# The first down-projection product of an encoder trunk: its right factors loaded anew for each of the seven products, and the attention carried on beside four of them

## The chip, the core and the metric

The kernel runs on one core of one Trainium2 chip. The metric is the device time in microseconds (us) of the whole program. Matmuls run on PE, elementwise work with two operands on DVE and POOL, activations and casts on ACT; SP issues nearly all DMAs. Each engine takes its own instructions strictly in the order in which they stand in its queue, and waits at an instruction until the semaphores that it needs are there. That order is written by the build: the kernel's Python yields pieces of work, two generators are woven into each other by weights, and a scheduler places the instructions of that stream into the five queues.

## The reference, cut to what matters

One layer, sequence of 2048 tokens, width 1024, float32:

```
h = rmsnorm(x); proj = h @ w_in
y_a = s5_mixer(..)            # state space
y_b = diff_attention(..)      # 6 heads, two softmax maps each, causal by chunks of 64
y_c = hgrn2_mixer(..)         # gated linear recurrence, 6 heads
x = x + concat(y_a, y_b, y_c) @ w_out
h = rmsnorm(x)
up = causal_conv3(h @ w_up) + conv_b; gate = h @ w_gate
x = x + (gelu(up) * gate) @ w_down      # 2816 -> 1024
return rmsnorm(x)
```

Every float32 matmul is done as three float16 matmuls on a high and a low half (the helper `split`: ACT makes the high half, DVE or POOL subtracts it for the low half).

## The kernel before, in words

**Stages.** In order of time: the input projection and the S5 part; then the gated recurrence (hgrn, tiles `g_...`) with the first rows of the attention beside it; `early_mix` (`o_pe`), a part of the output projection; and `phase_tail`, which works on two halves of 1024 tokens each. For the first half the tail does the output projection (`project`, `o_pm`), the normalisation and transposes (`o_pt`), the up and gate products (`activations`, `f_pm`, 1848 matmuls), and the down-projection (`Down`, `f_pd`). Then `second` does the output projection of the second half, `activations` and `Down` follow for it, and the program ends.

**The attention.** `phase_attn` is called twice: for query blocks 0 to 7, and for blocks 8 to 15 (the "second part"). One row is one block of 128 queries of one head. A row with block number i has L = 128(i+1) keys. Its steps: score matmuls `t_ps` (PE, line 834, 3 or 4 per map in the second part, two maps), a biased copy with running maximum on DVE (line 838, one for each `t_ps`), the exponentials on ACT (line 850, two of 128 x L), the difference of the two maps on DVE (line 869), the cast on ACT (line 892), the low half on POOL (line 893), two transposing DMAs on SP (line 900, `t_wt`), and the value matmuls `t_po` (PE, line 915, 64 columns each, three for each block of 128 keys). The second part has 48 rows and 336 `t_ps`.

**The weave.** `weave(fore, 1.0, right(), 1.0)` draws from the attention (`left`) or from all else (`right`), whichever has the smaller account. A piece of the attention's second part adds its n times `LW[4]` times `K.pace`; a piece of the tail adds n times `LW[5]` = 1. `K.pace` is 1.0 at first, 1.8 from the output projection on, and is set again where `activations` begins. `run(fore)`, handed down as `ahead`, draws what is left of the attention at one go.

**The down-projection.** `Down` computes (1024 x 2816) @ (2816 x 1024) as seven products of half size (a Strassen-like scheme). Product i needs a left factor (sums of the activations, written to the DRAM tensor `Ad` by `factors`, read back as `f_da` by `left`) and a right factor (a sum of the four quarters B11, B12, B21, B22 of `w_down`, split into the float16 pair `f_dw`). A product runs over four parts c of 3, 3, 3 and 2 blocks (`DOWN_PARTS`), 36, 36, 36 and 24 matmuls, 132 in all, into four PSUM banks; at its end `put` adds them to the rows `f_r` on DVE (line 1750). There are six buffers for parts of right factors, so one and a half products are held at a time.

For the first half (`staged` = 4) the right factors of products 0 to 3 come by `stage`: the quarter is loaded in pieces of at most two blocks into the pool `f_dst` (3 buffers of 512 KB), for product 3 two quarters are loaded and subtracted on POOL, then split. Ahead of product 2, `before()` draws the rest of the attention, and `hold` opens the pool `f_db` for the four whole quarters. They are loaded there (line 1726), and products 4 to 6 form their factors from what lies there, each sum overwriting one quarter (lines 1730 and 1733, POOL). Product 6 of the first half is left to `second`. For the second half all right factors come from held quarters.

**Lines that the prediction touches.** 834, 838, 850, 869, 892, 893, 900, 915: a row of the attention. 98: the `f_pm` matmuls. 60 and 58: the low half of an activation factor `f_a` on DVE and on POOL. 62: the low half of a weight. 1705 and 1726: loads into `f_dst` and `f_db`. 1743: load of `f_da`. 1772: the `f_pd` matmuls. 1837: the helper `add`.

Of the kernel before, what the change touches and what calls it, by code (L numbers as in the profile page):

```python
# [26 lines left out]
CH = 512  # L27
# [9 lines left out]
LW = [6.0, 0.44, 5.0, 2.5, 0.62, 1.0]  # L37
# [1383 lines left out]
def phase_tail(K, x, Xd, Yd, Ad, w_out, norm_g, W, conv_w, conv_b, w_down, final_g, out, es,  # L1421
# [228 lines left out]
    class Down:  # L1650
# [19 lines left out]
        LOADS = ({2: (B12, B11), 3: (B22,), 4: (B21,)}, {0: (B21,), 1: (B22, B11), 2: (B12,)})  # L1670
# [22 lines left out]
        def stage(self, i, st, cs=(0, 1, 2, 3)):  # L1693

            for c in cs:
                q0, n = self.cuts[c]
                w = self.room(i, c)
                for q in range(0, n, 2):
                    k = min(2, n - q)
                    b, pair, _ = self.STEPS[i]  # L1700
                    fs = []
                    for b in pair or (b,):
                        f = st.tile([128, KD, 128], F32, tag="wst", name="f_dst")
                        f = f.rearrange("p (q a) f -> p q (a f)", q=2)[:, 0:k]
                        nc.sync.dma_start(out=f, in_=self.source(b, q0 + q, k))
# [96 lines left out]
        def run(self, rs, tp, pms, side, staged, before):  # L1802
# [3 lines left out]
            with ExitStack() as e1:  # L1806
                pool = pooler(e1)
                st = pool("f_dst", 3) if staged > 1 else None
                self.more(pool)
                if not self.w:  # L1810
                    self.ahead(st)
                with ExitStack() as e2:
                    for i in range(6):
# [3 lines left out]
                        if i == staged - 1 - (staged > 1):  # L1817
                            before()
                            self.hold(pooler(e2)("f_db", 1, side))
                        for b in self.LOADS[self.half].get(i, ()):  # L1820
                            self.load(b)
                        if i + 1 < staged:
                            self.stage(i + 1, st)
                        else:
                            for c in range(len(self.cuts)):
                                if i + 1 == staged == 4:
                                    self.sum(3, c)
                                self.right(i + 1, c)
# [3 lines left out]
                if self.half == 1:  # L1832
                    yield from self.product(6, pms[6 % len(pms)], True)
            self.last = self.product(6, pms[0], False)
# [76 lines left out]
    def first(pm):  # L1911

        with ExitStack() as e1:
# [22 lines left out]
            K.pace = 1.0  # L1936
# [45 lines left out]
    with ExitStack() as e2:  # L1982
# [7 lines left out]
        yield from down.run(total(0), tp, [pm], "left", 4, ahead)  # L1990
# [9 lines left out]
    yield from down.run(total(1), tp, [pd, pm], "left", 1, lambda: None)  # L2000
# [117 lines left out]
```

## Time and profile before

| what | value |
|---|---|
| median of 3 runs | 2815.44 us (2808.53 to 2818.59) |
| the profiled execution: time | 2795.69 us |
| the profiled execution: span of the instructions | 2794.0 us |
| mean granted clock of PE | 0.931 of full speed |

The page gives shares of the whole span. For this change the shares of single stages count, and those come from the view that cuts the span into windows. In its rows stand the length of the window, the busy time of each engine with the number of its instructions in brackets, the granted PE clock, the mean busy share of the DMA engines and the GB/s that they moved. Matmuls overlap: one of 512 columns is recorded with about 0.38 us, but the next starts about 0.22 us after it, so the rate is read from counts in a window.

### The profile page before, as it was taken

To read this page: it belongs to the slowest core of one execution; us is meant where nothing else is said; L and a number is where in the kernel's file an instruction comes from. 1 tells how busy PE (TensorE), PEld (TensorE's weight loads), DVE (VectorE), ACT (ScalarE), POOL (GpSimd) and SP (SyncE) were. 2 spreads that over 40 slices of the span, in tenths; PEclk is the share of its full clock that TensorE was granted. 3 is DMA by queue.
4 is the path that set the end of the run, shared out by engine and by line. 5 is a ranking of instruction groups with operands and counts; after the bars stand their busy time and mean duration, and the time that the engine had idled before them with its cause. 6 is when DMAs were issued, how large, how long until landed. Compare 5 with 4: busy or idle time off the path is not lost. (4 is left out here: it accounts for less than half of the span.)

```text
span 2794.0 us, 42749 instructions
## 1 busy us (share of the span) xinstructions
PE 2442.0 (87%) x15438; PEld 1375.0 (49%) x15438; DVE 2004.2 (72%) x3893; ACT 1222.2 (44%) x2231; POOL 1309.4 (47%) x1095
## 2 busy tenths in 40 slices
PE   5998897989988888677998887859899999999998
PEld 3654546867766764243443333324344444444443
DVE  7466746789988897688779899975654855555575
ACT  5333344556645663565345555552234422222221
POOL 4788602334334432246666666631802344444180
PEclk8999998989989988788999999979999999999999
DMA  6675554555464656864455655587775655554733
GB/s 226 232 219 192 162 174 101 123 131 132 90 150 98 132 130 134 253 171 120 164 172 158 175 140 159 142 256 239 258 268 192 221 164 154 166 155 143 270 103 121
DMA packets 554533, 474.13 MB, mean 170 GB/s; under 512 B 276880, under 2 KB 432848, under 8 KB 553296
## 3 DMA queue, kind: packets, MB, share of 16 engines
q1 hardware_dynamic: 532144, 431.02, 54.1%
q10 hardware_dynamic: 22176, 40.38, 4.0%
q8 instruction: 121, 1.98, 0.3%
q14 instruction: 92, 0.75, 0.1%
HBM read 289.30 MB, written 127.93 MB: 149 GB/s over the span
## 5 line engine op out<-in xcount | busy, mean ns | idle before, releaser
L98 PE MATMUL f_pm<-f_q,f_w 128*128 128x512 f16 x3696 | 841.3, 387 | 37.9 <-DVE f_u L1837 21.7
L98 PEld LDWEIGHTS <-f_w 128*128 128x128 f16 x3696 | 363.7, 99 | 506.7 <-issue 90.4
L1772 PE MATMUL f_pd<-f_dw,f_da 128*128 128x512 f16 x1848 | 406.5, 383 | 11.7 <-DVE f_r L1750 10.4
L893 POOL TENSOR_TENSOR t_sc<-t_sc 128x1024 f16<-128x1024 f32 (+7 forms) x144 | 250.2, 1749 | 338.9 <-ACT t_sc L892 313.5
L1772 PEld LDWEIGHTS <-f_da 128*128 128x128 f16 x1848 | 181.8, 99 | 233.0 <-issue 18.5
L850 ACT ACTIVATE t_sc<-t_sc,t_nm 128x128 f32<-128x128 f32 (+7 forms) x192 | 229.1, 1195 | 99.1 <-DVE t_nm L845 91.7
L834 PE MATMUL t_ps<-t_k,t_q 96*128 96x512 f16 (+2 forms) x480 | 168.7, 377 | 99.0 <-DVE t_mx L838 86.6
L838 DVE CUSTOM_DVE_ANT_0 t_sc<-t_ps,t_base,t_mx 128x512 f32<-128x512 f32 (+3 forms) x288 | 185.1, 643 | 28.2 <-PE t_ps L834 21.5
L60 DVE TENSOR_TENSOR f_a<-f_t,f_a 128x512 f16<-128x512 f32 x132 | 148.1, 1129 | 46.1 <-ACT f_a L54 42.0
L98 PE MATMUL g_pq<-g_h,g_w 128*128 128x256 f16 x1152 | 158.6, 298 | 16.7 <-DVE g_sg L1162 10.6
L915 PE MATMUL t_po<-t_v,t_wt 128*128 128x64 f16 x2448 | 123.2, 201 | 56.4 <-DMA t_wt<-t_sc 48.7
L915 PEld LDWEIGHTS <-t_wt 128*128 128x128 f16 x2448 | 109.2, 104 | 123.1 <-DMA t_wt<-t_sc 67.0
L1837 POOL TENSOR_TENSOR f_t<-f_t,f_t 128x512 f32<-128x512 f32 x66 | 106.8, 1632 | 129.3 <-ACT f_a L54 108.3
L1487 PE MATMUL o_pm<-o_w,o_y 128*128 128x512 f16 x624 | 147.1, 394 | 19.9 <-DMA o_y<-Yd 14.1
L869 DVE SCALAR_TENSOR_TENSOR t_sc<-t_sc,t_a 128x1024 f32<-128x1024 f32 (+7 forms) x144 | 163.2, 1159 | 0.9
L1837 POOL TENSOR_TENSOR f_k<-f_k,f_k 128x512 f32<-128x512 f32 x88 | 124.7, 1417 | 73.2 <-ACT f_k L1869 68.3
L98 PE MATMUL g_pv<-g_w,g_h 128*128 128x256 f16 x1152 | 151.5, 288 | 8.0 <-ACT g_w L54 4.7
L62 DVE SCALAR_TENSOR_TENSOR f_dw<-f_db,f_dw 128x1536 f16<-128x1536 f32 (+1 forms) x36 | 104.1, 2910 | 73.8 <-ACT f_dw L54 73.7
L1837 POOL TENSOR_TENSOR f_db<-f_db 128x1536 f32<-128x1536 f32 (+1 forms) x32 | 128.2, 4044 | 60.6 <-DMA f_db<-in_w_down_dram 60.6
L892 ACT CAST t_sc<-t_sc 128x1024 f16<-128x1024 f32 (+7 forms) x144 | 112.1, 793 | 93.1 <-DVE t_sc L869 89.5
L54 ACT ACTIVATE f_w<-f_sum 128x512 f16<-128x512 f32 x110 | 69.2, 629 | 182.4 <-DVE f_sum L141 76.9
L54 ACT ACTIVATE f_a<-f_t 128x512 f16<-128x512 f32 x154 | 95.5, 628 | 114.5 <-POOL f_t L1837 56.6
(327 smaller groups left out, 4534.8 us busy)
## 6 DMA issues: line engine op xcount, KB each, us to landing
f_w<-Wd SPq DMA_DIRECT2D x231, 256.0 KB, 3.0
Wd<-f_w SPq DMA_DIRECT2D x154, 256.0 KB, 2.1
Ad<-f_a ACTq DMA_DIRECT2D x154, 256.0 KB, 2.8
f_da<-Ad SPq DMA_DIRECT2D x42, 768.0 KB, 4.4
g_h<-Hd SPq DMA_DIRECT2D x24, 1024.0 KB, 7.0
f_db<-in_w_down_dram SPq DMA_DIRECT2D x24, 768.0 KB, 10.5
o_wst<-in_w_out_dram SPq DMA_DIRECT2D x32, 512.0 KB, 5.4
o_y<-Yd SPq DMA_DIRECT2D x52, 256.0 KB, 4.7
```

Of the source, the lines that this page charges most:

```text
L54: nc.scalar.activation(out=hi, in_=src, func=AF.Copy, scale=scale)
L60: nc.vector.tensor_tensor(out=lo, in0=src, in1=hi, op=ALU.subtract)
L98: nc.tensor.matmul(out=out, lhsT=lhs(a, k), rhs=rhs(b, k), start=(n == 0), stop=(n == 3 * nk - 1))
L834: nc.tensor.matmul(out=ps[:, 0:k1 - k0], lhsT=qt[:, c, 128 * (i % 4):128 * (i % 4) + 128], rhs=H.k[:, c, k0:k1], start=True, stop=True,)
L838: V.tensor_tensor_reduce(out=sc[c][:, k0:k1], in0=ps[:, 0:k1 - k0], in1=bs[:, k0:k1], scale=1.0, scalar=-3e38 if j == 0 else mx[:, c, j - ...
L850: nc.scalar.activation(out=sc[c][:, 0:L], in_=sc[c][:, 0:L], func=AF.Exp, scale=SLOPES[h], bias=nm[:, c:c + 1], accum_out=H.la[:, c, n_:n_ ...
L869: V.scalar_tensor_tensor(out=sc[0][:, k0:k1], in0=sc[1][:, k0:k1], scalar=a[:, 1:2], in1=sc[0][:, k0:k1], op0=ALU.mult, op1=ALU.add,)
L893: nc.gpsimd.tensor_tensor(out=hl[:, LM + k0:LM + k1], in0=sc[0][:, k0:k1], in1=hl[:, k0:k1], op=ALU.subtract,)
L915: nc.tensor.matmul(out=po, lhsT=wt[:, w, b, :], rhs=vt[:, b, 64 * v:64 * v + 64], start=(b == 0 and w + v == 0), stop=(b == i and w == 1),)
L1487: nc.tensor.matmul(out=ps[t], lhsT=y[:, k, a, 128 * t:128 * t + 128], rhs=w[:, b, k, :], start=(q == qs[0] and i == 0), stop=(q == qs[-1] ...
L1772: nc.tensor.matmul(out=ps[t], lhsT=a[:, q, x, tk], rhs=w[:, y, q, :], start=(first and q + x + y == 0), stop=(last and q == n - 1 and y == 1),
L1837: eng.tensor_tensor(out=o, in0=a, in1=b, op=op)
```

## The change

`Down.run` is parted in two. The first half's product gets its own function `streamed`: all seven right factors come by `stage`, in pieces, from `w_down`. The table `SUMS` says which quarters a factor is made of: one for products 0, 1, 2, two for 3 and 4, three for 5. For product 5 the sum is kept as one tile (`f_db`, a quarter of the space that `hold` took), and product 6 takes its factor from that and B21. The pool `f_dst` has 4 buffers instead of 3. The rest of the attention is drawn ahead of product 4 instead of product 2. Quarters read for the first half: 11 instead of 9 (each 1408 x 512 float32, 2.88 MB). The second half's `run` is as before with the cases for the first taken out. `LW[4]` goes from 0.62 to 0.72, and `K.pace` beside `activations` from 1.0 to 0.86, so that their product there stays (0.619 for 0.62), while beside the recurrence and the output projection the attention's account grows faster.

```diff
-LW = [6.0, 0.44, 5.0, 2.5, 0.62, 1.0]
+LW = [6.0, 0.44, 5.0, 2.5, 0.72, 1.0]
...
+        SUMS = (
+            (B11,), (B21,), (B22,), (B12, B11), (B22, B12), (B22, B12, B11), (B21,),
+        )
+
+        def stage(self, i, st, kept=None):
...
-                    for b in pair or (b,):
+                    for b in self.SUMS[i]:
                         f = st.tile([128, KD, 128], F32, tag="wst", name="f_dst")
                         f = f.rearrange("p (q a) f -> p q (a f)", q=2)[:, 0:k]
                         nc.sync.dma_start(out=f, in_=self.source(b, q0 + q, k))
                         fs.append(f)
                     f = fs[0]
-                    if pair:
+                    if i == 6:
+                        add(f, kept[:, q0 + q:q0 + q + k], f, ALU.subtract, P)
+                    elif len(fs) > 1:
                         add(f, f, fs[1], ALU.subtract, P)
+                    if i == 5:
+                        t = kept[:, q0 + q:q0 + q + k]
+                        add(t, f, fs[2])
+                        f = t
                     K.split(w[:, 0, q:q + k], w[:, 1, q:q + k], f, WS)
...
+        def streamed(self, rs, tp, pm, before):
...
+                st = pool("f_dst", 4)
                 self.more(pool)
+                self.ahead(st)
+                kept = None
+                for i in range(6):
+                    for c in range(len(self.cuts)):
+                        if (i, c) not in self.a:
+                            self.left(i, c)
+                    if i == 4:
+                        before()
+                        kept = e1.enter_context(
+                            tc.tile_pool(name="f_db", bufs=1, side="left", reuse_waits="tile")
+                        ).tile([128, MF // 2, CH], F32, name="f_db")
+                    self.stage(i + 1, st, kept)
+                    yield from self.product(i, pm, False)
+            self.last = self.product(6, pm, False)
...
-            K.pace = 1.0
+            K.pace = 0.86
             yield from activations(hc, 0, pooler(e1), pm, 1, 3, 5, 3, None)
...
-        yield from down.run(total(0), tp, [pm], "left", 4, ahead)
+        yield from down.streamed(total(0), tp, pm, ahead)
...
-    yield from down.run(total(1), tp, [pd, pm], "left", 1, lambda: None)
+    yield from down.run(total(1), tp, [pd, pm], "left")
```

What the build makes of it shows in the queues. The first place is ACT at the end of the recurrence: `g_yo` is its last output, `o_w` the first weight of the tail's output projection, line 850 the exponentials of a row of the attention, whose second size tells its L. Before:

```order
L850 ACTIVATE t_sc,t_la<-t_sc,t_nm 128x1664 x2
L850 ACTIVATE t_sc,t_la<-t_sc,t_nm 128x1792 x2
L892 CAST t_sc<-t_sc 128x1024
L892 CAST t_sc<-t_sc 128x640
L54 ACTIVATE g_yo<-g_py,g_gc 128x512
L892 CAST t_sc<-t_sc 128x1024
L892 CAST t_sc<-t_sc 128x768
L54 ACTIVATE o_w<-o_wst 128x1024
L850 ACTIVATE t_sc,t_la<-t_sc,t_nm 128x1920 x2
```

In the change:

```order
L850 ACTIVATE t_sc,t_la<-t_sc,t_nm 128x1280 x2
L54 ACTIVATE g_yo<-g_py,g_gc 128x512
L892 CAST t_sc<-t_sc 128x1024
L892 CAST t_sc<-t_sc 128x256
L54 ACTIVATE t_yo<-t_pt,t_gc 128x512
...
L850 ACTIVATE t_sc,t_la<-t_sc,t_nm 128x1408 x2
L54 ACTIVATE o_w<-o_wst 128x1024
L850 ACTIVATE t_sc,t_la<-t_sc,t_nm 128x1536 x2
```

Where the row of 1792 keys stood ahead of `g_yo`, that of 1280 keys stands now: the attention is four rows behind there. Counted over PE's queue, the `t_ps` that stand ahead of a place are:

| place in PE's queue | before | change |
|---|---|---|
| first matmul of `early_mix` | 261 | 248 |
| last matmul of `early_mix` | 284 | 268 |
| first matmul of the tail's output projection | 306 | 282 |
| first up and gate matmul | 341 | 326 |
| last up and gate matmul of the first half | 465 | 444 |
| first matmul of product 0 | 480 | 466 |
| first matmul of product 4 | 480 | 480 |

And 174 `t_po` instead of 48 stand behind the first matmul of product 0.

The second place is POOL between the activations' last factors and the first sum for a right factor: `f_t` are the last two tiles of activations, `f_a` the last factor's low half, `t_sc` the attention's, `f_dst` the first sum. Before:

```order
L1837 TENSOR_TENSOR f_t_19546<-f_t_19797,f_t_19546 128x512
L893 TENSOR_TENSOR t_sc<-t_sc 128x1024
L893 TENSOR_TENSOR t_sc<-t_sc 128x768
L1837 TENSOR_TENSOR f_t_19797<-f_t_19797,f_t_19546 128x512
L893 TENSOR_TENSOR t_sc<-t_sc 128x1024
L893 TENSOR_TENSOR t_sc<-t_sc 128x896
L58 TENSOR_TENSOR f_a<-f_t_19797,f_a 128x512
L893 TENSOR_TENSOR t_sc<-t_sc 128x1024 x2
L1837 TENSOR_TENSOR f_dst<-f_dst 128x1024
```

In the change:

```order
L1859 TENSOR_TENSOR f_t_19304<-f_t_19547,f_t_19304 128x512
L1859 TENSOR_TENSOR f_t_19547<-f_t_19547,f_t_19304 128x512
L893 TENSOR_TENSOR t_sc<-t_sc 128x1024
L893 TENSOR_TENSOR t_sc<-t_sc 128x512
L58 TENSOR_TENSOR f_a<-f_t_19547,f_a 128x512
L893 TENSOR_TENSOR t_sc<-t_sc 128x1024
L893 TENSOR_TENSOR t_sc<-t_sc 128x640
L893 TENSOR_TENSOR t_sc<-t_sc 128x1024
L893 TENSOR_TENSOR t_sc<-t_sc 128x768
L1859 TENSOR_TENSOR f_dst<-f_dst 128x1024
```

Two attention casts stand ahead of the last `f_a` where there were four.

The third place is SP's queue around products 4 and 5: `f_da<-Ad_74` are the left factors of product 4, `Ad_75` those of product 5. Before:

```order
L1726 DMA f_db<-in_w_down_dram 128x3x512 x3
L1726 DMA f_db<-in_w_down_dram 128x2x512
L1743 DMA f_da<-Ad_74 128x3072 x3
L1743 DMA f_da<-Ad_74 128x2048
L1726 DMA f_db<-in_w_down_dram 128x3x512 x3
L1726 DMA f_db<-in_w_down_dram 128x2x512
L1743 DMA f_da<-Ad_75 128x3072 x3
L1743 DMA f_da<-Ad_75 128x2048
```

In the change:

```order
L1753 DMA f_da<-Ad_74 128x2048
L1472 DMA o_y<-Yd 128x2x512 x4
L1753 DMA f_da<-Ad_75 128x3072
L950 DMA Yd<-t_yo 256x1x512 x2
L1709 DMA f_dst<-in_w_down_dram 128x2x512 x3
L1709 DMA f_dst<-in_w_down_dram 128x512
L1753 DMA f_da<-Ad_75 128x3072
L1474 DMA o_wst<-in_w_out_dram 128x2x512 x2
L1709 DMA f_dst<-in_w_down_dram 128x512 x2
L1709 DMA f_dst<-in_w_down_dram 128x2x512
L1753 DMA f_da<-Ad_75 128x3072
L1753 DMA f_da<-Ad_75 128x2048
```

The pieces of product 5's right factor stand between loads of its left factor, each of which waits for a part of product 4, and behind the attention's last stores (`Yd<-t_yo`). From the up and gate products of the second half on, the queues of all engines are as before.

More of the change, by code (lines that the diff above doesn't have):

```diff
@@ L1667, in phase_tail @@
         )
-        LOADS = ({2: (B12, B11), 3: (B22,), 4: (B21,)}, {0: (B21,), 1: (B22, B11), 2: (B12,)})
+        LOADS = {0: (B21,), 1: (B22, B11), 2: (B12,)}
         def __init__(self, half, pool):
@@ L1691, in room @@
             return w
-        def stage(self, i, st, cs=(0, 1, 2, 3)):
-            for c in cs:
-                q0, n = self.cuts[c]
+        SUMS = (
+            (B11,), (B21,), (B22,), (B12, B11), (B22, B12), (B22, B12, B11), (B21,),
+        )
+        def stage(self, i, st, kept=None):
+            for c, (q0, n) in enumerate(self.cuts):
                 w = self.room(i, c)
@@ L1699, in stage @@
                     k = min(2, n - q)
-                    b, pair, _ = self.STEPS[i]
                     fs = []
-                    for b in pair or (b,):
+                    for b in self.SUMS[i]:
                         f = st.tile([128, KD, 128], F32, tag="wst", name="f_dst")
@@ L1800, in product @@
                 yield 2.5 * self.cuts[c][1]
-        def run(self, rs, tp, pms, side, staged, before):
+        def streamed(self, rs, tp, pm, before):
             self.rs, self.tp = rs, tp
@@ L1807, in run @@
                 pool = pooler(e1)
-                st = pool("f_dst", 3) if staged > 1 else None
+                st = pool("f_dst", 4)
                 self.more(pool)
-                if not self.w:
-                    self.ahead(st)
+                self.ahead(st)
[12 more added lines that the diff above has]
+            self.last = self.product(6, pm, False)
+        def run(self, rs, tp, pms, side):
+            self.rs, self.tp = rs, tp
+            with ExitStack() as e1:
+                pool = pooler(e1)
+                self.more(pool)
                 with ExitStack() as e2:
@@ L1816, in run @@
                                 self.left(i, c)
-                        if i == staged - 1 - (staged > 1):
-                            before()
+                        if i == 0:
                             self.hold(pooler(e2)("f_db", 1, side))
-                        for b in self.LOADS[self.half].get(i, ()):
+                        for b in self.LOADS.get(i, ()):
                             self.load(b)
[L1822 to L1828, printed above, removed]
+                        for c in range(len(self.cuts)):
+                            self.right(i + 1, c)
                         if i < 5:
@@ L1831, in run @@
                 yield from self.product(5, pms[5 % len(pms)], False)
-                if self.half == 1:
-                    yield from self.product(6, pms[6 % len(pms)], True)
-            self.last = self.product(6, pms[0], False)
+                yield from self.product(6, pms[6 % len(pms)], True)
     def add(o, a, b, op=ALU.add, eng=V):
```

## The prediction, as put on record

> **What bounds the kernel now.** I read the windows by stage first, then who stands still between them. PE is busy for most of the span, but not evenly:
>
> ```profile
> span 2794.0 us, 42749 instructions
> PE 2442.0 (87%) x15438; PEld 1375.0 (49%) x15438; DVE 2004.2 (72%) x3893; ACT 1222.2 (44%) x2231; POOL 1309.4 (47%) x1095
> ...
> core 0: us, PE busy (x) PEld busy (x) DVE busy (x) ACT busy (x) POOL busy (x), PEclk, DMA share, GB/s
> 800.00:1100.00 300.00, 260.83 (x2469) 191.09 (x2468) 262.18 (x655) 164.22 (x276) 112.74 (x90) 0.89 0.57 125
> 1140.00:1260.00 120.00, 95.80 (x620) 50.48 (x620) 86.50 (x188) 72.96 (x135) 41.28 (x27) 0.86 0.80 226
> 1300.00:1400.00 100.00, 93.40 (x446) 42.10 (x445) 75.02 (x85) 35.49 (x66) 69.81 (x48) 1.00 0.53 175
> 1400.00:1800.00 400.00, 338.27 (x1930) 156.46 (x1928) 352.02 (x541) 215.41 (x356) 260.11 (x167) 0.94 0.55 157
> 1815.00:1862.00 47.00, 16.54 (x152) 8.70 (x151) 39.75 (x70) 26.11 (x38) 19.97 (x12) 0.62 0.81 241
> 1862.00:1992.00 130.00, 120.74 (x584) 54.78 (x583) 58.31 (x71) 33.42 (x47) 44.79 (x18) 0.97 0.81 273
> 1992.00:2052.00 60.00, 58.82 (x265) 26.34 (x266) 47.59 (x34) 16.13 (x18) 36.60 (x9) 0.97 0.56 192
> ```
>
> In the recurrence (800 to 1100) and in the activations beside the attention (1400 to 1800) DVE is busy for 87 and 88 of 100 us and PE falls behind. In products 0 to 3 of the down-projection (1862 to 1992) it is the other way: PE 93 of 100, DVE 45. So a row of the attention costs DVE time where DVE is short, and would cost PE time in the products. How much it costs beside the activations shows when their matmuls and the score matmuls are counted:
>
> ```profile
> 1300.00:1400.00 100.00, 92.76 (x425) 14.31 (x21) 8.62 (x15) 1.00 0.53 175
> 1400.00:1800.00 400.00, 307.21 (x1270) 40.69 (x61) 26.37 (x46) 0.94 0.55 157
> ...
> 800.00:1100.00 300.00, 50.61 (x140) 92.64 (x140) 0.89 0.57 125
> 1400.00:1800.00 400.00, 35.45 (x102) 65.94 (x100) 0.94 0.55 157
> ...
> 800.00:1100.00 300.00, 135.37 (x180) 96.92 (x120) 68.44 (x39) 0.89 0.57 125
> ```
>
> The first two rows are the `f_pm` alone, the next two the `t_ps`, the last what touches `t_sc` in the recurrence (DVE, ACT, POOL). With the attention nearly silent, 425 `f_pm` go through in 100 us. At that rate 1270 need 299 us; they took 400, with 102 `t_ps`. So one `t_ps`, with its share of its row, costs 101/102, about 1.0 us. In the recurrence it holds DVE for 135.37/140 = 0.97 us. The two agree: **about 1 us for each `t_ps` that leaves a stage in which DVE is short.**
>
> **The change part by part.** The queue counts in the section on the change give five terms.
>
> *The recurrence.* At the end of `early_mix` 16 fewer `t_ps` stand, at the first matmul of the tail 24. The 16 lie where DVE is short: 16 x 0.97 = 15.5 us off. The other 8 lie in the change of stage from 1100 to 1140, in which DVE is busy for 24 of 40 us and waits much for transfers:
>
> ```profile
> 1100.00:1140.00 40.00, 18.29 (x139) 8.64 (x137) 24.45 (x68) 13.52 (x23) 12.19 (x7) 0.62 0.61 109
> ...
> 1140.61 3.43 PE L1487 MATMUL o_pm<-o_w,o_y 128*128 128x512 f16 x8 [3.24 <-ACT o_w L54]
> ```
>
> There I take 0.3 us each. Together **-18 us**; bounds: -23 (all 24 at full price) and -4 (the recurrence is held by its own chain).
>
> *The output projection.* 9 more `t_ps` (44 for 35). DVE is 72% busy there and the DMA engines 80%; between 0 and 9 us, I take **+4**.
>
> *The activations.* 118 `t_ps` for 124, the weight per piece the same: 6 x 1.0, **-6** (0 to -9).
>
> *From the last `f_pm` to product 0.* PE stands still here, because the factor pool reuses the memory of the activations, so that its first load waits for the last `f_a`, and that chain is shared with the attention:
>
> ```profile
> 1816.12 1.03 PE L98 MATMUL f_pm<-f_q,f_w 128*128 128x512 f16 x4
> ...
> 1833.35 5.92 DVE L60 TENSOR_TENSOR f_a<-f_t,f_a 128x512 f16<-128x512 f32 x3
> ...
> 1847.86 4.41 POOL L893 TENSOR_TENSOR t_sc<-t_sc 128x1024 f16<-128x1024 f32 x2 [9.14 <-ACT t_sc L892]
> 1852.24 1.15 POOL L58 TENSOR_TENSOR f_a<-f_t,f_a 128x512 f16<-128x512 f32 x1
> ...
> 1853.85 3.03 SPq L1705 DMA_DIRECT2D f_dst<-in_w_down_dram  x3
> ...
> 1861.95 31.33 PE L1772 MATMUL f_pd<-f_dw,f_da 128*128 128x512 f16 x132 [1.25 <-ACT f_dw L54]
> ```
>
> The last `f_a` on POOL starts right at the end of the attention's 4.41 us, and the load follows its end. The change has two such casts fewer ahead of it (-4.4 us), but 12 biased copies of line 838 instead of 4 between the last `f_a` on DVE and the first split. From 1400 to 1800 DVE spent 65.94 us on 100 of them, 0.66 each, so 8 more are 5 to 6 us; the load's own 8 us (1853.85 to 1861.95) hides most of it. I take **-4**, between -9 and +7.
>
> *Products 0 to 5.* To PE come 14 `t_ps` and 126 `t_po`, the work of three rows. The first row below is that of the `t_po` alone, then come products 3 to 5 on PE, then a transposing DMA of the one row that runs there now:
>
> ```profile
> 1862.00:1992.00 130.00, 1.89 (x48) 0.51 (x5) 0.97 0.81 273
> 1960.12 30.05 PE L1772 MATMUL f_pd<-f_dw,f_da 128*128 128x512 f16 x132 [5.46 <-DVE f_r L1750]
> 1993.18 58.83 PE L1772 MATMUL f_pd<-f_dw,f_da 128*128 128x512 f16 x264 [3.02 <-DVE f_r L1750]
> ...
> 1869.96 4.29 SPq L900 DMA_TRANSPOSE t_wt<-t_sc  x1
> ```
>
> A matmul of 512 columns takes 58.83/264 = 0.22 us, a value matmul 1.89/48 = 0.04: 14 x 0.22 + 126 x 0.04 = 8 us. DVE's part, three rows of 8 x 0.97 us, finds 72 idle us in products 0 to 3; ACT (33 of 130 us busy) and POOL (45) have room too. Six more transposing DMAs stand in SP's queue among the loads, and each waits there for the row's casts, at 4.3 us as the one above up to 26 us of SP in 130; the loads behind them have a product's lead, so I take 3 us of waiting for them. Off go the 5.5 us that PE waits at product 3: its factor of two quarters runs through three buffers one piece at a time, seven pieces from
>
> ```profile
> 1917.31 2.34 POOL L1837 TENSOR_TENSOR f_dst<-f_dst 128x1024 f32<-128x1024 f32 x1 [48.35 <-DMA f_dst<-in_w_down_dram]
> 1954.78 2.34 POOL L1837 TENSOR_TENSOR f_dst<-f_dst 128x1024 f32<-128x1024 f32 x1 [6.45 <-DMA f_dst<-in_w_down_dram]
> ```
>
> that is 37.5 us for six steps where a product takes 29 (132 x 0.22). With four buffers two pieces are on their way. New is product 5's factor: three tiles a piece, four buffers, so again one piece at a time, and its chain can start only some 12 us into product 4, since its first sums stand on DVE behind the attention's last `t_yo`, whose transposes stand on PE behind 44 matmuls of product 4 (44 x 0.22 = 10 us, and the split of `t_yo`). Its last part is needed when 108 matmuls of product 5 are done: 29 + 24 = 53 us after product 4 began, 41 us after the chain did. By then five pieces must follow the first two. At 37.5/6 = 6.2 us a piece plus a third transfer, about 8 us, that is 40. It just fits, and I take 4 us of waiting: 8 + 3 - 5.5 + 4, **+9** (from -3, nothing waits any more, to +47, rival A).
>
> The transfers in this stretch:
>
> ```profile
> GB/s 247 275 239 352 273 302 279 315 120 151 211 365 254 228 184 157 291 153 246 371 398 387 401 402 397 270 167 261 392 72 166 158 8 169 230 321 166 107 169 224
> DMA packets 23096, 46.93 MB, mean 247 GB/s; under 512 B 5488, under 2 KB 7024, under 8 KB 23085
> ...
> f_dst<-in_w_down_dram SPq DMA_DIRECT2D x18, 512.0 KB, 4.3
> f_db<-in_w_down_dram SPq DMA_DIRECT2D x12, 768.0 KB, 11.9
> ```
>
> Two more quarters are 5.77 MB, at the 400 GB/s of the best slices 14 us of transfers, in 190 us that run at 247 GB/s on the mean: covered, if the queue spreads them. The Trainium skill (DMA: Bandwidth & Descriptors, Specifications) gives about 358 GB/s as what memory grants one core; by it the same bytes take an estimated 16 us, and uncovered they would bring the sum to +1 instead of -1; eight slices here moved more than that, so I keep the row, and by neither does it bind at the mean.
>
> At nothing I cost the second half's new `run` (same queues), the 21 or so DMA issues more on SP, and the kept tile.
>
> **The sum**: -18 + 4 - 6 - 4 + 9 = -15 us, from 2795.69 to 2780.7 for a profiled execution. That execution lies 20 us under the median of the runs; I carry the difference over: 2815.4 - 15 = **2800 us**. What a measurement of this kernel can tell from no change is about 0.3%, 8 us.
>
> **The rivals.**
>
> *A. Product 5 waits for its factor: slower.* Place: products 4 and 5. In the queue before, the 512 KB loads into `f_dst` land in 4.3 us, but those into `f_db`, issued in a crowd, in 11.9. At 11.9 each of the five pieces is 7.6 us longer: 38 us of waiting more, sum +23, 2838 us. It decides from about 8 us of landing on (5 x 3.8 = 19 us more than I allow). For it: SP issues in order, and the pieces stand behind loads that wait for parts of product 4 and beside `o_y` and `o_wst`. Against: in products 0 to 3 the pieces did land in 4.3 us at 273 GB/s. A second thing lengthens the same chain:
>
> ```profile
> L62 DVE SCALAR_TENSOR_TENSOR f_dw<-f_dst,f_dw 128x1024 f16<-128x1024 f32 x20 | 25.7, 1287 | 37.5 <-ACT f_dw L54 37.5
> L62 DVE SCALAR_TENSOR_TENSOR f_dw<-f_db,f_dw 128x1024 f16<-128x1024 f32 x9 | 23.8, 2639 | 16.4 <-ACT f_dw L54 16.3
> ```
>
> The same split takes twice as long where POOL works on `f_db`. The rows bound the price: 1.35 us for each of five pieces, 7 us. The Trainium skill (SBUF — State Buffer, Who interferes with whom) says why: a DVE instruction with two SBUF inputs and a POOL instruction that reads SBUF exclude each other for a whole instruction; by it a sum or split may wait out a full POOL subtraction of 2.34 us, an estimated 12 us for five pieces, instead of the 7 of the rows, and no run so far shows which. I give the rival 0.20.
>
> *B. Nothing to gain in the recurrence: the same.* If the chain of the recurrence and not DVE sets its pace, the first term is -4, the sum -1, 2814 us. For it: PE is 87% busy there as well, at a clock of 0.89. Against: the price of 1.0 us beside the activations is DVE's time almost to the number. Chance 0.22.
>
> *C. All terms at their better ends*: -23 + 0 - 7 - 6 + 0 = -36, 2779 us: the products swallow the rows in DVE's idle time and the stall at product 3 goes without a new one. Chance 0.16.
>
> That the rows do not move at all is out: the queues show it.
>
> **How the numbers follow.** The forecast of 2800 us has 0.42; with C, faster by over 0.3% comes to 0.58. B makes the 0.22 within 0.3%, A the 0.20 slower. The range from 2777 to 2828 holds C, the forecast, B and the milder part of A (waits up to 25 us more than allowed); the rest of A and something beyond C are left out. The likeliest case's own range is 2788 to 2807.
>
> **What would show it right or wrong.** Right: the first `o_pm` at about 1122 instead of 1140.61; the last `f_pm` some 20 us earlier than 1816; from there to the first `f_pd` about 41 us instead of 45; products 0 to 5 in about 199 us instead of 190, with at most 7 us of waiting at the heads and parts of products. Wrong: an unmoved `o_pm` (B); or PE idle in product 5 behind ACT or DVE `f_dw`, with `f_dst` landing in over 8 us (A).

## The result and the profile after

The changed kernel takes 2789.94 us (median of 7 runs, 2775.5 to 2795.62), the kernel before 2807.1 us (7 runs, the three of the prediction among them). Over all these runs the ratio is **0.9923**, 95% interval 0.9898 to 0.9949; beside other kernels in a later session it was 0.9910 (0.9893 to 0.9926). In microseconds of the kernel before that is 22 and 25 less (the medians differ by 17 and 28), where the forecast said 15. Single executions scatter by 10 us to either side, and the profiled one of the kernel before (2795.69) lies below all its seven runs here. So the traces tell where the time went, and the ratios how much there is.

The page of the changed kernel, its span and its first part, and from its last part the load that has taken the place of the held quarters:

```profile
span 2773.6 us, 42851 instructions
PE 2437.3 (88%) x15438; PEld 1373.2 (50%) x15438; DVE 1984.2 (72%) x3909; ACT 1220.7 (44%) x2240; POOL 1294.1 (47%) x1100
f_dst<-in_w_down_dram SPq DMA_DIRECT2D x48, 512.0 KB, 4.8
```

The windows by stage, in the change: the recurrence, the activations without and with the attention, the passage to product 0, products 0 to 3, products 4 and 5. Columns as in the prediction.

```profile
800.00:1100.00 300.00, 265.19 (x2478) 195.60 (x2476) 244.17 (x640) 156.09 (x264) 109.90 (x88) 0.86 0.56 119
1300.00:1400.00 100.00, 90.62 (x414) 40.11 (x413) 69.55 (x78) 37.46 (x70) 67.03 (x46) 1.00 0.45 158
1400.00:1785.00 385.00, 326.93 (x1892) 152.82 (x1892) 349.36 (x532) 209.83 (x348) 251.46 (x161) 0.95 0.56 160
1786.00:1823.00 37.00, 15.32 (x122) 7.11 (x122) 29.94 (x70) 21.32 (x35) 15.88 (x11) 0.55 0.93 285
1823.00:1953.00 130.00, 123.13 (x658) 56.54 (x656) 82.40 (x113) 50.57 (x71) 51.70 (x23) 0.96 0.86 268
1953.00:2023.00 70.00, 67.19 (x356) 31.56 (x357) 35.66 (x49) 13.50 (x18) 20.09 (x11) 1.00 0.81 283
```

DVE has fallen from 262 to 244 us of the 300 in the recurrence (in the change this window takes in 17 us behind the last `g_po`), and risen from 58 to 82 of the 130 in products 0 to 3, where PE loses nothing by it (123 for 121). Beside the activations it is as full as before, 91 of 100.

From the first and last matmul of each stage on PE the lengths are, in us:

| stage | before | change | difference | change, later run | forecast |
|---|---|---|---|---|---|
| to the first `o_pm` | 1140.6 | 1114.9 | -25.7 | -22.2 | -18 (-23 to -4) |
| to the first `f_pm` | 112.5 | 114.3 | +1.8 | +2.3 | +4 (0 to +9) |
| to the last `f_pm` of the first half | 564.0 | 556.6 | -7.4 | -7.9 | -6 (-9 to 0) |
| to the first `f_pd` | 44.8 | 37.0 | -7.8 | -8.0 | -4 (-9 to +7) |
| products 0 to 5 | 190.1 | 199.7 | +9.6 | +14.3 | +9 (-3 to +47) |
| end of product 5 to product 6 | 96.2 | 103.3 | +7.1 | +9.6 | 0 |
| product 6 to the end | 645.8 | 647.8 | +2.0 | +2.3 | 0 |

Up to the end of product 5 the signs are all as forecast. The second output projection, behind it, lost 7 to 10 us that the forecast did not have. The column of the kernel before rests on one trace, and that one lies 11 us below the median.

### The profile page after: what moved, and what is told of

It reads as the page before. It is cut to its first block, busy times and chain, and to the rows that moved or that the text cites. A ratio compares the mean times of both kernels' runs of the same rounds, so it can differ in the third digit from the quotient of the medians.

```text
span 2773.6 us, 42851 instructions
## 1 busy us (share of the span) xinstructions
PE 2437.3 (88%) x15438; PEld 1373.2 (50%) x15438; DVE 1984.2 (72%) x3909; ACT 1220.7 (44%) x2240; POOL 1294.1 (47%) x1100
## 5 line engine op out<-in xcount | busy, mean ns | idle before, releaser
L893 POOL TENSOR_TENSOR t_sc<-t_sc 128x1024 f16<-128x1024 f32 (+7 forms) x144 | 255.8, 1789 | 345.4 <-ACT t_sc L892 298.5
L1782 PEld LDWEIGHTS <-f_da 128*128 128x128 f16 x1848 | 181.1, 98 | 225.2 <-issue 12.5
L60 DVE TENSOR_TENSOR f_a<-f_t,f_a 128x512 f16<-128x512 f32 x132 | 140.7, 1073 | 47.5 <-ACT f_a L54 42.9
L869 DVE SCALAR_TENSOR_TENSOR t_sc<-t_sc,t_a 128x1024 f32<-128x1024 f32 (+7 forms) x144 | 155.3, 1102 | 1.2
L98 PEld LDWEIGHTS <-g_w 128*128 128x128 f16 x1152 | 120.5, 107 | 46.5 <-issue 17.7
L838 DVE CUSTOM_DVE_ANT_0 t_sc<-t_ps,t_base 128x512 f32<-128x512 f32 (+2 forms) x192 | 120.6, 633 | 31.9 <-PE t_ps L834 22.6
```

The lines of the kernel that those rows point to most:

```text
L60: nc.vector.tensor_tensor(out=lo, in0=src, in1=hi, op=ALU.subtract)
L98: nc.tensor.matmul(out=out, lhsT=lhs(a, k), rhs=rhs(b, k), start=(n == 0), stop=(n == 3 * nk - 1))
L838: V.tensor_tensor_reduce(out=sc[c][:, k0:k1], in0=ps[:, 0:k1 - k0], in1=bs[:, k0:k1], scale=1.0, scalar=-3e38 if j == 0 else mx[:, c, j - ...
L869: V.scalar_tensor_tensor(out=sc[0][:, k0:k1], in0=sc[1][:, k0:k1], scalar=a[:, 1:2], in1=sc[0][:, k0:k1], op0=ALU.mult, op1=ALU.add,)
L893: nc.gpsimd.tensor_tensor(out=hl[:, LM + k0:LM + k1], in0=sc[0][:, k0:k1], in1=hl[:, k0:k1], op=ALU.subtract,)
L1782: nc.tensor.matmul(out=ps[t], lhsT=a[:, q, x, tk], rhs=w[:, y, q, :], start=(first and q + x + y == 0), stop=(last and q == n - 1 and y == 1),
```

## The experiments

**One part alone.** Two kernels halve the change. The first keeps the streaming and takes back the weights:

```diff
-LW = [6.0, 0.44, 5.0, 2.5, 0.72, 1.0]
+LW = [6.0, 0.44, 5.0, 2.5, 0.62, 1.0]
...
-            K.pace = 0.86
+            K.pace = 1.0
```

> The changed kernel with the attention's weights put back (LW[4] 0.62, pace 1.0 beside the activations): the right factors are streamed and the rest of the attention is drawn ahead of product 4, but by then nothing is left (480 t_ps stand ahead of product 0, as in the kernel before). Theory W (the weights gain: t_ps taken out of the recurrence and the change of stage behind it): at most the waits of 5.5 and 3.0 us at products 3 and 4 go, ratio to the kernel before 0.997 to 1.002, first o_pm of the first half at 1136 to 1145 us. Rival S (streaming gains: fewer crowded loads, no wait for held quarters): ratio 0.991 to 0.994, about the whole gain of the change.

Measured: ratio **1.0013** (0.9998 to 1.0029), first `o_pm` at 1147.7. The streaming alone gains nothing. Products 0 to 5 take 197.5 us, 7.4 more than before, though no row was added to them: product 3 begins 10.9 us after product 2 has ended (5.5 before), and product 5 7.1 us after product 4, where before it followed at once.

The second is the kernel before with the two numbers of the change and held quarters:

```diff
-LW = [6.0, 0.44, 5.0, 2.5, 0.62, 1.0]
+LW = [6.0, 0.44, 5.0, 2.5, 0.72, 1.0]
...
-            K.pace = 1.0
+            K.pace = 0.86
```

> The kernel before with only LW[4] 0.72 and pace 0.86: the same t_ps ahead of every stage up to product 0 as in the change (282 at the first o_pm, 466 at product 0), the rest drawn ahead of product 2, quarters held. Theory W: first o_pm at 1112 to 1118, product 0 some 35 us earlier than before, then 14 t_ps and 174 t_po with the crowd of held loads cost 10 to 20 us in products 0 to 3: ratio 0.991 to 0.996. Rival S: ratio 0.998 to 1.002, the stages ahead unmoved or their gain given back whole. Rival I (both are needed, the weights' gain is lost without the stream): first o_pm early, but products 0 to 5 over 225 us instead of 190.

Measured: ratio **0.9972** (0.9956 to 0.9988), a little above what theory W gave. The first `o_pm` comes at 1112.7 and product 0 at 1816.7, 45 us earlier than before; then products 0 to 5 take 226 us, which is rival I's number. So theories W and S fall as they stood, and I holds: the weights earn the time, and the streaming, worth nothing by itself, lets the kernel keep it. The place where it is lost is one row of PE in this kernel (in brackets the idle time ahead of the row and what ended it):

```profile
1977.26 3.14 PE L1772 MATMUL f_pd<-f_dw,f_da 128*128 128x512 f16 x7 [21.48 <-ACT f_dw L54]
```

The transfers of that time, from 1945 to 1985, in slices of 1 us:

```profile
GB/s 406 343 259 180 254 373 410 408 408 387 387 403 373 387 385 389 385 389 385 385 389 385 389 389 387 426 412 420 401 399 395 391 389 383 389 305 115 6 0 0
...
f_db<-in_w_down_dram SPq DMA_DIRECT2D x12, 768.0 KB, 12.7
```

Product 4 waits 21.5 us for its factor. The held quarters were first asked for at 1945.39, when product 3 had 10 us left. Its factor needs B12 and B22, the first and the third in the queue (`LOADS`): three quarters of 2.88 MB, which at 390 GB/s are 22 us. A transfer at full rate, then, that began too late. (The Trainium skill, Perfetto Trace Analysis, Roofline, puts the ceiling of a core whose neighbour is idle at about 435 GB/s, above the 358 that the prediction gave beside its row; the slices, of 426 at most, agree with it.)

**Why the held quarters begin late.** In that kernel their first load stands right behind the attention's last store in SP's queue, so either the queue holds them or the memory does. Here the stores go out by ACT:

```diff
-                nc.sync.dma_start(out=Yd[2 + h // 2, :, :, c0:c0 + CH], in_=o)
+                nc.scalar.dma_start(out=Yd[2 + h // 2, :, :, c0:c0 + CH], in_=o)
```

> The kernel before with LW[4] 0.72 and pace 0.86 (held quarters, as in the second run, which gave 0.9972 and a wait of 21.5 us ahead of product 4) and the stores of the attention's outputs issued by ACT instead of SP. It asks why the held quarters come late there. Theory Q (their loads stand in SP's queue behind the attention's last two stores): the first load goes out 8 to 15 us earlier, the wait ahead of product 4 falls to under 10 us, ratio to the kernel before 0.990 to 0.994. Rival M (the held quarters lie in memory that the attention's tiles give back only at their end, whoever issues the stores): the wait stays at 15 to 25 us, the first load goes out only after the last t_yo on DVE, ratio 0.995 to 0.999.

Measured: ratio 0.9949 (0.9932 to 0.9967), at the edge of rival M; the wait ahead of product 4 stays, 21.2 us. What SP's queue waits for between 1925 and 1990 in this kernel (total, times, longest, us) decides it:

```profile
SPq L1726 <- DMA Yd<-t_yo: 13.1, 2, 8.8
SPq L1743 <- PE f_pd L1772: 10.9, 2, 6.9
...
SPq L1726 <- DMA f_da<-Ad: 0.9, 1, 0.9
```

The stores are in another queue now, and line 1726, the load into `f_db`, still waits for them, 13.1 us in two pieces: the tiles of `f_db` lie where `t_yo` lay. (That M had the first load behind the last `t_yo` on DVE was too strict: six went out from 1949.47 on, the others from 1968.) Theory Q falls, M holds. In the change no load into `f_dst` waits for such a store, in 62 waits of line 1709 between 1823 and 2030 (three of them, 5.1 us, are put down to other tiles of the attention); so the streamed factors can begin while rows of the attention still run.

**Where the rest of the attention is drawn.** Ahead of product 2 instead of 4:

```diff
-                    if i == 4:
+                    if i == 2:
                         before()
+                    if i == 4:
                         kept = e1.enter_context(
```

> The changed kernel with the rest of the attention drawn ahead of product 2, as before, instead of product 4; all else as in the change. If the spreading of rows over four products is worth something (theory D), products 2 and 3 stretch by more than in the change (36.4 us the longest there) and the ratio to the kernel before is 0.995 or above. If not (theory W, where only the stage the rows leave matters), the ratio is that of the change within 0.3%: 0.990 to 0.995.

Measured: ratio **0.9897** (0.9875 to 0.9919), just below theory W's range; theory D fell. The rows now crowd into product 2, 44 us long, and products 0 to 5 take 197.3 us all the same. Later this kernel and the change were timed side by side:

> The changed kernel once more, beside the next two on the same chip. Its ratio was 0.9923, 0.9898 to 0.9949. Expected 0.990 to 0.994; its second output projection (end of product 5 to product 6), 103.5 us in its profile, again over 100 us if theory D is right (the rest drawn ahead of product 4 pushes the loads of the second projection), 92 to 104 us as in the other kernels if that time only scatters.

> The changed kernel with the rest of the attention drawn ahead of product 2 once more, beside the change. Theory D (that place is better by 0.3%, from the second projection): ratio to the kernel before lower than the change's of the same call by 0.002 to 0.004. Rival (the place doesn't matter, the two first results scattered): within 0.0015 of it.

Measured: the change 0.9910 (0.9893 to 0.9926), the other 0.9886 (0.9866 to 0.9906). Lower by 0.0026 the first time and 0.0024 now, with intervals that overlap: probably 0.25% better, not more than that can be said. That the second projection is the cause is not shown: it took 103.3 and 105.8 us in the change, 96.4 and 104.1 with the earlier place. One part of it did fall both times: PE's waits for the loads of `o_y` there were 16.8 and 18.5 us in the change, 11.2 and 12.5 with the earlier place. The two times of the latter differ with the granted clock, 1.00 in the run of 96.4 us and 0.93 in that of 104.1.

**The fourth buffer.**

```diff
-                st = pool("f_dst", 4)
+                st = pool("f_dst", 3)
```

> The changed kernel with 3 buffers in the factor pool f_dst instead of 4. If the streaming needs the fourth buffer (product 5's three-tile sums fill a pool of three), products 4 and 5 wait for their factors: 10 to 30 us, ratio to the kernel before 0.996 to 1.003. If three do (loads land in 4.7 us and the pieces come in time), the ratio is that of the change within 0.002.

Measured: ratio **0.9949** (0.9931 to 0.9967), against 0.9910 for the change beside it: 11 us, just outside the ratio I gave and inside the microseconds. Product 5 in this kernel, whose sums take three tiles at once:

```profile
2002.67 2.11 PE L1782 MATMUL f_pd<-f_dw,f_da 128*128 128x512 f16 x9
2005.05 13.76 PE L1782 MATMUL f_pd<-f_dw,f_da 128*128 128x512 f16 x63
2022.74 4.48 PE L1782 MATMUL f_pd<-f_dw,f_da 128*128 128x512 f16 x20
2027.64 3.61 PE L1782 MATMUL f_pd<-f_dw,f_da 128*128 128x512 f16 x16 [0.41 <-ACT f_dw L54]
2038.57 7.01 PE L1782 MATMUL f_pd<-f_dw,f_da 128*128 128x512 f16 x24 [2.26 <-ACT f_dw L54]
```

It lasts 42.9 us instead of 31.9. The holes between the rows are partly filled by `o_pm`, so the brackets show only 2.7 of them.

**What a row costs in each stage.** More rows are moved from the activations into the products:

```diff
-            K.pace = 0.86
+            K.pace = 1.0
```

> The changed kernel with pace 1.0 instead of 0.86 beside the activations: the recurrence and the output projection as in the change (282 t_ps at the first o_pm, 326 at the first f_pm), but 420 instead of 444 t_ps ahead of the last f_pm of the first half and 56 instead of 14 beside products 0 to 3. By the price of 1.0 us for a t_ps beside the activations the stage gets 24 us shorter. Theory W with free products: they take the rows in idle time of DVE, ratio to the kernel before about 0.984. Rival P (products charge as much as they did in the change, about 10 us for 14 t_ps, 0.7 each): 24 less 29, ratio 0.993 to 0.996.

Measured: ratio 0.9991 (0.9973 to 1.0009). The activations took 532.6 us instead of 556.6: 24.0 us for 24 `t_ps`, the price of 1.0 (the stage took 556 to 559 us in all other traces with 118 to 123 `t_ps` there). But products 0 to 5 took 260 us instead of 200, twice rival P's 29. At the head of product 5 PE, then SP:

```profile
2013.37 10.73 PE L1782 MATMUL f_pd<-f_dw,f_da 128*128 128x512 f16 x36 [7.15 <-ACT f_dw L54]
...
2006.91 4.64 SPq L950 DMA_DIRECT2D Yd<-t_yo  x2
2012.26 1.93 SPq L1709 DMA_DIRECT2D f_dst<-in_w_down_dram  x4
```

The attention now ends only behind product 4, and PE finishes product 4 at 1981.0 and begins product 5 at 2013.4. In between lies the end of the last row, and the pieces of product 5's factor stand behind its two stores in SP's queue. So the products take a dozen `t_ps` cheaply and more of them dearly: the first 14 cost 2 to 7 us against the streaming alone (197.5 us), the next 42 another 60, and 32 us lie in this gap.

The other way, out of the recurrence and into the activations, with product 0 unchanged at 466 `t_ps`:

```diff
-LW = [6.0, 0.44, 5.0, 2.5, 0.72, 1.0]
+LW = [6.0, 0.44, 5.0, 2.5, 0.9, 1.0]
...
-                    if i == 4:
+                    if i == 2:
                         before()
+                    if i == 4:
...
-            K.pace = 0.86
+            K.pace = 0.6
```

> The changed kernel with the rest of the attention drawn ahead of product 2, LW[4] 0.9 and pace 0.6 beside the activations: 255 t_ps ahead of the last o_pe (268 in the change), 264 ahead of the first o_pm (282), 305 ahead of the first f_pm (326), 442 and 466 ahead of the last f_pm and of product 0 (444 and 466 in the change). So 18 t_ps move from the recurrence and the change of stage to the activations, nothing else. Price theory (0.8 us for a t_ps in the recurrence, 2 in the change of stage, 1.0 beside the activations): 13 x 0.8 and 5 x 2 come to 20 us off at the first o_pm, 19 t_ps more beside the activations give back 19: ratio to the kernel before as with the same place of the rest and the weights of the change, 0.988 to 0.992. Rival R (the recurrence keeps gaining, the activations swallow rows for less): 0.980 to 0.986. Rival L (the tail of the recurrence is by now bound by its own chain): 0.993 to 0.998.

Measured: ratio **0.9937** (0.9915 to 0.9958), in rival L's range and just beside the price theory's. The activations, from the first `f_pm` to the last, with the window's columns as above:

```profile
1228.60:1806.50 577.90, 483.12 (x2717) 224.11 (x2715) 506.35 (x776) 291.71 (x500) 375.30 (x242) 0.94 0.54 156
```

577.9 us, against 557.5 with 19 `t_ps` fewer: 1.07 each, as said. The first `o_pm` came at 1105.9, only 10 to 15 us earlier than in the two runs of the kernel beside it (1116.2 and 1121.0) where I said 20, and the output projection, 112.2 and 113.1 us there, gave about 10 of it back (122.7 us, at a granted clock of 0.81, 0.87 in the first of the two). What holds that stage is not settled.

**The change of stage.**

```diff
-LW = [6.0, 0.44, 5.0, 2.5, 0.72, 1.0]
+LW = [6.0, 0.44, 5.0, 2.5, 0.62, 1.0]
...
-            K.pace = 0.86
+            K.pace = 1.0
...
-            for _ in phase_hgrn(K, Hd, w_in, hgrn_lb_logits, hgrn_norm_g, Yd, spare):
-                yield LW[3]
+            for k, _ in enumerate(phase_hgrn(K, Hd, w_in, hgrn_lb_logits, hgrn_norm_g, Yd, spare)):
+                yield LW[3] if k < 230 else 0.5
```

> The changed kernel with LW[4] 0.62 and pace 1.0, and the last 21 pieces of the recurrence counted at 0.5 instead of 2.5: 278 t_ps ahead of the last o_pe (284 in the kernel before, 268 in the change) and 305 ahead of the first o_pm, so 27 t_ps stand in the change of stage instead of 22 (before) or 14 (change). Read is only the time from the end of the last o_pe to the first o_pm: 39.1 us before, 22.6 in the change. Theory G (the rows of the attention that stand in the last chain of the recurrence, g_po to g_yo to o_y, delay it by about 2 us per t_ps): 46 to 52 us. Rival F (the gap has a length of its own and differs by where the last row happens to end): 36 to 42 us. Forecast's price of 0.3 us per t_ps: 40 to 41 us.

Measured, in the one execution that there is: 44.7 us, between theory G and rival F. Neither stands, and the rows show why: the mark was badly chosen. Before, PE at the end of the recurrence and then DVE's last step of it:

```profile
1097.48 1.46 PE L1409 MATMUL o_pe<-o_we,o_ye 128*128 128x512 f16 x6
1098.78 2.75 PE L1409 MATMUL o_pe<-o_wx,o_ye 128*128 128x512 f16 x12
1103.69 0.68 PE L1328 MATMUL g_po<-g_st,g_qh 64*64 64x64 f32 x18
...
1129.18 0.74 DVE L62 SCALAR_TENSOR_TENSOR g_yo<-g_py,g_gc,g_yo 128x512 f16<-128x512 f32 x1
```

In the change:

```profile
1082.69 0.68 PE L1328 MATMUL g_po<-g_st,g_qh 64*64 64x64 f32 x18
1083.40 1.46 PE L1409 MATMUL o_pe<-o_we,o_ye 128*128 128x512 f16 x6
1084.70 2.75 PE L1409 MATMUL o_pe<-o_wx,o_ye 128*128 128x512 f16 x12
1088.23 1.46 PE L1409 MATMUL o_pe<-o_we,o_ye 128*128 128x512 f16 x6
1089.53 2.75 PE L1409 MATMUL o_pe<-o_wx,o_ye 128*128 128x512 f16 x12
...
1094.62 0.75 DVE L62 SCALAR_TENSOR_TENSOR g_yo<-g_py,g_gc,g_yo 128x512 f16<-128x512 f32 x1
1114.93 3.32 PE L1487 MATMUL o_pm<-o_w,o_y 128*128 128x512 f16 x9
```

The recurrence does not end with the last `o_pe` but with the last `g_po`, and from there the way runs over `g_yo` and its store to the loads of `o_y` and the first `o_pm`, with rows of the attention between them in every queue. Before, all 144 `o_pe` stand ahead of that `g_po`. In the change 36 of them, 8.4 us of PE, stand behind it, beside the 11.2 us that pass from `g_po` to `g_yo` (24.8 before, where ACT had rows of 1664 and 1792 keys ahead of `g_yo`). By the right mark there are 18 `t_ps` fewer ahead of the last `g_po`, which ends at 1083.4 instead of 1104.4, and 15 instead of 21 behind it, where the way to `o_pm` is 31.5 us instead of 36.2. In this experiment it is 24 `t_ps` and 41.1 us, and in the one before, 12 and 30.9. Read off these four kernels, a `t_ps` behind `g_po` costs little up to 15, 0.8 us from there to 21, and 1.6 beyond; that is a line through four points, and other things change sides with them.

**The stores in another queue.** The change, and the kernel with the earlier place, each with the attention's stores issued by ACT (the edit stands above):

> The changed kernel with the stores of the attention's outputs (Yd from t_yo) issued by ACT instead of SP, so that nothing waits behind them in SP's queue. Theory Q (in the change SP's order, with the factor pieces of product 5 and the loads of the second output projection behind the attention's last stores, costs 7 to 10 us): the second projection, from the end of product 5 to product 6, shrinks from 103 to about 96 us, ratio to the kernel before 0.988 to 0.991. Rival B (the loads of the second projection wait for bandwidth or for buffers of the factor pool, not for the stores): no gain, 0.991 to 0.995.

> The same stores on ACT, and the rest of the attention drawn ahead of product 2 as in an earlier run (which gave 0.9897 with the stores on SP). By theory Q there is little left to gain, since there the stores already stand ahead of products 3 to 5: 0.988 to 0.991. If the stores delay SP wherever they stand, 0.983 to 0.987.

Measured: 0.9893 (0.9875 to 0.9910) and 0.9885 (0.9864 to 0.9907). The first is in theory Q's range, yet its reason fell: the second projection took 104.6 us, no less than the 103.3 of the change. The moved stores also shift the rows by a few (463 instead of 466 `t_ps` ahead of product 0), the output projection is 7 us shorter than in the change and the passage to product 0 is 4. What gains is open, and the second, where the stores already stood early, is at 0.9885 the same as its parent.

## Why the forecast was right, and where its steps failed

- **The gain comes from the rows that leave the recurrence: right.** The first `o_pm` is 22 to 26 us earlier in the change, 28.0 with the weights alone, and 7 later with the streaming alone. Single traces scatter, but the queues help: up to there the kernel with the streaming alone has every queue of the kernel before, and four others here have every queue of the change. From the last matmul that PE's queue shares (it ends between 922 and 928 us) to the first `o_pm` it is 217 and 221 us with the old weights, and 189 to 193 in the seven traces with the new. Rival B is out.
- **Its size and its place: wrong.** The bound of -23 was passed in one trace (-25.7) and nearly reached in the other (-22.2); counted from the shared matmul it is 23 to 32. The step that failed is the split at the last `o_pe`: "16 x 0.97 = 15.5 us off" in front of it and "0.3 us each" behind it. Measured by that split it was 6 to 9 in front and 16 behind. I had counted `t_ps` alone. The queues also show that 36 `o_pe` change sides with the last `g_po`, so that their 8.4 us go into the shadow of the recurrence's last chain. At most those 8.4 us of the 22 to 26 are due to that; no run takes them apart from the rows. Nearest is the kernel with `LW[4]` at 0.9: with the same 36 behind, 15 `t_ps` fewer brought the last `g_po` 8 to 14 us forward beside the two traces of its kernel at 0.72, 0.6 to 1.0 each. With these rows gone DVE is no longer the fuller engine: from the shared matmul to the last `g_po` it was busy for 160 of 180 us before and for 129 of 161 in the change, PE for 157 and 143. That this is why a later row earns less than 0.97 is likely, but not shown.
- **The output projection, the activations and the passage: right in sign.** The activations' price of 1.0 us per `t_ps` was confirmed from both sides (24.0 us for 24, 20.4 for 19). The passage gained 8 where I had 4, near the end of its bound, and where I looked for it: the last `f_a` on POOL ends 28.8 us after the last `f_pm` instead of 36.2, and from there to product 0 it is 8.2 us instead of 8.6.
- **Products 0 to 5: +9 forecast, +9.6 and +14.3 measured.** The number came out, the working did not. I had 8 us of rows on PE and 1.5 us more of waiting. PE's busy time (the first figure behind the window's length), in the kernel before, the change and the streaming alone:

```profile
1861.95:2052.01 190.06, 179.62 (x849) 81.17 (x849) 105.97 (x104) 49.61 (x65) 81.38 (x26) 0.97 0.73 247
1822.85:2022.53 199.68, 190.00 (x1013) 88.01 (x1012) 118.06 (x163) 63.75 (x89) 71.33 (x34) 0.97 0.84 273
1873.67:2071.18 197.51, 184.92 (x875) 83.53 (x875) 107.37 (x124) 52.94 (x76) 64.47 (x31) 0.96 0.79 271
```

In the change PE is busy for 10.4 us more and idle for 0.7 less (2.6 more in the later run). Of its work some 5 us are 23 matmuls `o_pm` of the second output projection, which now run among the products, where none did before; the sum had no term for them. The streaming alone, with no `t_ps` in the products, brings 26 of them in and takes 7.4 us more than the kernel before, so that by these single traces only 2 to 7 us are left for the rows. Of the waits, those at the heads of products 4 and 5 are short: product 4 follows product 3 within 0.2 us (3.02 before) and product 5 product 4 within 1.6. The 5.5 us at product 3 did not go: it begins 7.7 us after product 2 has ended, and 10.9 us after it with the streaming alone. What is late there in the change is the attention itself in PE's queue:

```profile
1909.99 5.34 PE L1782 MATMUL f_pd<-f_dw,f_da 128*128 128x512 f16 x24
1923.00 5.68 PE L1782 MATMUL f_pd<-f_dw,f_da 128*128 128x512 f16 x18
...
1959.55 9.66 PE L1782 MATMUL f_pd<-f_dw,f_da 128*128 128x512 f16 x44
```

PE's waits between 1823 and 2030 in the change (total, times, longest):

```profile
PE t_ps L834 <- DVE t_mx L838: 6.5, 2, 5.5
PE t_po L915 <- DMA t_wt<-t_sc: 2.9, 2, 1.8
```

In the 7.7 us between the end of product 2 (1915.3) and the start of product 3 PE stands behind a `t_ps` that waits 5.5 us for DVE; of the products' own waits only 0.2 us are left in the list.
- **Rival A, a late factor for product 5: did not come, and is real.** The loads land in 4.8 us, the row of the page says. With three buffers, or with the attention running until product 5, product 5 lasted 43 and 45 us. The longer chain that A also feared is only a little longer: the split that reads the kept tile, and POOL's subtractions beside it, between 1970 and 2030 in the change:

```profile
L1859 POOL TENSOR_TENSOR f_dst<-f_db,f_dst 128x1024 f32<-128x1024 f32 x4 | 11.5, 2886 | 1.0 <-issue 1.0
L62 DVE SCALAR_TENSOR_TENSOR f_dw<-f_db,f_dw 128x1024 f16<-128x1024 f32 x4 | 6.2, 1550 | 3.9 <-ACT f_dw L54 3.9
```

  1.55 us instead of 1.29, 0.3 more for a piece and not the 1.35 of my bound. Two of the four began while POOL was at a subtraction, and the rows show what that costs:

```profile
2002.20 1.27 POOL L1859 TENSOR_TENSOR f_dst<-f_dst 128x512 f32<-128x512 f32 x1 [3.17 <-DMA f_dst<-in_w_down_dram]
2002.91 1.64 DVE L62 SCALAR_TENSOR_TENSOR f_dw<-f_db,f_dw 128x1024 f16<-128x1024 f32 x1 [1.12 <-ACT f_dw L54]
...
2014.11 2.50 POOL L1859 TENSOR_TENSOR f_dst<-f_db,f_dst 128x1024 f32<-128x1024 f32 x1 [0.97 <-issue]
2015.58 2.11 DVE L62 SCALAR_TENSOR_TENSOR f_dw<-f_db,f_dw 128x1024 f16<-128x1024 f32 x1 [1.18 <-ACT f_dw L54]
```

  Both splits end 1.08 us after the subtraction that ran when they began: of their 1.64 and 2.11 us, 0.56 and 1.03 are waiting. The other two, which met none, took 1.23 each. The rule of the Trainium skill (SBUF — State Buffer, Who interferes with whom), by which I estimated 12 us for five pieces, holds for both pairs that met; the estimate was too high because only two did, for 1.3 us in all.
- **The sum: -15 forecast, -22 and -25 by the ratios.** Over the first four terms the traces are 12 to 15 us better than forecast. Part of that was spent in the second output projection, +7 and +10, for which the sum had no term. The queues that I called unchanged begin only behind it, with the up and gate products of the second half. PE in that stage, from the end of product 5 to product 6, and what it waits for there, in the kernel before and in the change:

```profile
2052.01:2148.23 96.22, 88.77 (x417) 41.15 (x415) 49.62 (x100) 38.73 (x71) 8.53 (x6) 0.98 0.72 252
2022.53:2125.84 103.31, 86.54 (x393) 39.69 (x392) 57.21 (x110) 43.17 (x81) 16.09 (x10) 0.92 0.70 244
...
PE o_pm L1487 <- DMA o_y<-Yd: 7.5, 5, 2.8
PE o_pm L1487 <- DMA o_y<-Yd: 16.8, 4, 6.5
```

  The stage lies between 91 and 106 us over all kernels here, at 103 and more in the change both times. PE waits 9.3 us longer for the loads of `o_y` (11.0 in the later run). It is busy only 2.2 us less, though 23 `o_pm` have already run beside the products: the granted clock of the stage fell from 0.98 to 0.92. Why these loads come later is open. In SP's queue the last six loads into `f_dst` (2013.17 to 2025.30) stand right ahead of four of them (2025.40), but no run moved them, and neither the place of the rest of the attention nor the queue of the stores moved the stage's length reliably.
- **What was luck.** That the sum came so near is in part chance: a front that gained 12 to 15 us more than forecast stands against a stage that lost 7 to 10 and had no term. Case C of the prediction also does not add up as it is named: at the better ends of its own bounds the sum is -23 + 0 - 9 - 9 - 3 = -44, not -36.

Of the kernels here the best are the change with the rest of the attention drawn ahead of product 2 (0.9897 and 0.9886), with or without the stores on ACT (0.9885). They beat the kernel before clearly, and the change probably, by about a quarter of a per cent.

## What to carry to other kernels

A change in two parts can have no gain in either: here one part earned the time and the other alone could keep it, because it broke a tie of memory (held tiles in the place of an earlier stage's last tile) that no queue shows and only the issuing queue's waits do. When work is moved away from a stage, look for the chain that ends the stage and count everything that changes sides with its last instruction, not only what was meant to move. And price a row of work by the stage that it enters as well: 1.0 us where DVE was full, little for the first dozen beside a full PE, and dear as soon as the next transfers stand behind it.

## What was not expected of the hardware

Twelve loads of 768 KB, issued in a crowd, kept the transfers between 373 and 426 GB/s for 30 us, each landing in 12.7 us at the median; loads of 512 KB spread over the products landed in 4.8 us. A landing time 2.6 times as long, for loads half as large again, was here no sign of a slow path: the transfers ran at about 390 GB/s, and each load shared that with those issued beside it.
